# Rewriting the opening of a conditioned decoder trunk: half of the modulation in column groups on TensorE, splits off GpSimd, one queue of transfers, instructions in written order

## The chip, the cores and the metric

The kernel runs on one core of a Trainium2 chip. The time is device microseconds of one execution of the whole program. Five engines work side by side on their own queues: TensorE (PE; its weight loads are shown apart as PEld), VectorE (DVE), ScalarE (ACT), GpSimd (POOL) and SyncE (SP, which here only issues transfers).

## The reference

One layer with a sequence of 1024 and a width of 1024, all float32:

```
mod = silu(c) @ ada_w + ada_b            # (1, 3*1024): shift, scale, gate
h = rms_norm(x, norm_w) * (1 + scale) + shift
proj = h @ w_in                          # all inputs of both mixers
y_h = hgrn2_branch(...)                  # 8 heads, gated linear recurrence
y_g = gla_branch(...)                    # 4 heads, gated linear attention
merged = sigmoid(mg0) * (y_h @ w_branch0) + sigmoid(mg1) * (y_g @ w_branch1)
out = rms_norm(x + gate * (merged @ w_out), final_norm_w)
```

The change concerns only how the program begins: the shift and scale, `h`, and the first six column groups of `proj` (four of q, two of k of the linear attention).

## The kernel before

`h` is kept transposed: eight tiles, one for each group of 128 channels `d`, 1024 positions wide, worked on in two halves of 512 positions. Every product is split: a float32 operand is rounded to a high part (`hi`, a cast on ACT) and the rest (`lo`, a subtraction), and a matmul becomes three, hi·hi, lo·hi and hi·lo. One 128x128 by 128x512 matmul of these is called a product below.

The opening does this for the first half of the positions:

- `load_x` brings four tiles of x, `norm_x` squares them on ACT, takes the root, and scales them on DVE; `transpose_x(half, xs, d)` turns channel group d with four TensorE matmuls against `ident` into `pm`, and ACT copies the result into `hT`.
- `load_mod(d0, nd)` brings the columns of `ada_w` that make shift and scale of `nd` channel groups. There are five blocks, (0,1), (1,1), (2,2), (4,2), (6,2) as (first d, how many). `make_mod` multiplies each of the eight row groups k with the column `cs[:, k]` of silu(c) and adds them up on DVE into `acc` (which lies in the tile `scT`); matmuls with a column of ones then sum over the partitions, and DVE makes `modv` and `amul`. In block 0 the first four k are done by 128x1 matmuls on TensorE instead (`on_pe`).
- `make_h(half, d)` applies scale and shift on ACT in place, splits the result into `h_hi[d]` and `h_lo[d]`, and every second d stores a pair to DRAM from POOL's queue.
- `load_wg(k)` brings one row group of the six weight columns, 128x768, into one of three buffers in `xb`; `prep_wg` splits it into `wa_*` and `wb_*`, casts on ACT, subtractions on POOL.
- For each d, 18 products go into six PSUM banks `accs` (four in `pd`, two in `sc_ps`): 144 for the half. They are started once per bank at d = 0 and stopped at d = 7.

Then `make_ga(0)` makes a small projection with 16-column matmuls in four column groups, `qk_out` moves the six banks out on DVE, and `first_group` does the second half's 144 products, bank by bank, while the main stream of later projections begins. In `first_group`'s third step (`i == 2`) `make_ga(1)` runs and the side track `alpha_side` starts; the attention that needs its results starts when the fourth job's values are there.

Up to `norm_x(0)` the instructions of PE, ACT and DVE stand in the order in which the code is written (`manual_schedule`, left by `order.close()`). After it a scheduler places them on each engine. `S.get` and `S.free` hand out 46 slots of 4 KB a partition in turn, so a transfer can wait for the last reader of its slot.

Of the kernel before, what the change touches and what calls it, by code (L numbers as in the profile page):

```python
# [82 lines left out]
def hybrid_trunk_kernel(  # L83
# [37 lines left out]
    one_t = ones[:, 0:1]  # L121
    ones_r = cp.tile([P, P], F32R, name="ones_r")
# [40 lines left out]
    nc.vector.tensor_mul(cs, cs, vec[:, R_C:R_C + 8])  # L163

# [22 lines left out]
    def split(src, hi=None, lo=None, eng=None, pin=False):  # L187
# [4 lines left out]
        i = nc.scalar.copy(hi, src)  # L192
        if pin:
            tc.keep_in_program_order(i)
        (eng or nc.vector).tensor_sub(lo, src, hi.bitcast(F32))  # L195
        return hi, lo
# [23 lines left out]
    def make_h(half, d):  # L220
        b = hT[half, d // 2][:, d % 2, :]
        sl = slice(half * 512, half * 512 + 512)
        nc.scalar.activation(b, b, AF.Identity, bias=modv[:, 0, d:d + 1], scale=amul[:, d:d + 1])
        split(b, h_hi[d][:, sl], h_lo[d][:, sl])
        if d % 2:
            nc.gpsimd.dma_start(h_d[half][d // 2], hT[half, d // 2].rearrange("p a t -> p (a t)"))

    def load_mod(d0, nd):
        kq = 4 // nd
        parts = []  # L230
        for kk in range(KT // kq):
# [5 lines left out]
            parts.append(b)  # L237
        return parts

    def make_mod(d0, nd, parts, on_pe):  # L240
        kq = 4 // nd
        acc = scT_f[:, (d0 // 2 % 2) * 512:(d0 // 2 % 2) * 512 + 2 * nd * P].rearrange("p (a f) -> p a f", a=2)
        for k in range(on_pe, KT):
            src = parts[k // kq][:, k % kq]
            if k == on_pe:
                i = nc.vector.tensor_scalar_mul(acc, src, cs[:, k:k + 1])
                if on_pe:
                    tc.keep_in_program_order(i)
            else:
                nc.vector.scalar_tensor_tensor(acc, src, cs[:, k:k + 1], acc, ALU.mult, ALU.add)  # L250
        pm = mtile()
        for half in range(2):
            for i in range(nd):
                o = pm[:, half * nd + i:half * nd + i + 1]
                for k in range(on_pe):
                    nc.tensor.matmul(o, parts[k // kq][:, k % kq, half, i * P:(i + 1) * P], cs[:, k:k + 1],
                                     start=(k == 0), stop=False)
                nc.tensor.matmul(o, acc[:, half, i * P:(i + 1) * P], one_t, start=(on_pe == 0), stop=True)
        S.free(*parts)
# [17 lines left out]

    def load_wg(k):
        raw = xb_f[:, (k % 3) * 768:(k % 3) * 768 + 768]
        nc.sync.dma_start(raw, w_in[0, k * P:(k + 1) * P, C_GQ:C_GQ + NG * P])  # L280
        return raw

    def prep_wg(k, raw):
        split(raw[:, 0:512], wa_hi[k // 2][:, k % 2, :], wa_lo[k // 2][:, k % 2, :], nc.gpsimd, k < 2)
        split(raw[:, 512:768], wb_hi[k // 4][:, k % 4, :], wb_lo[k // 4][:, k % 4, :], nc.gpsimd, k < 2)
# [23 lines left out]
    blocks = [(0, 1), (1, 1), (2, 2), (4, 2), (6, 2)]  # L309
    mods, raws = {}, {}  # L310

    def load_mods(bi):
        mods[bi] = load_mod(*blocks[bi])

    def load_w(k):
        raws[k] = load_wg(k)

    for bi in range(3):
        load_mods(bi)
        load_w(bi)  # L320
    norm_x(0, x_t)
    vec_rows(rows_a, 24, R_SH)
    order.close()
    make_mod(0, 1, mods.pop(0), 4)
    transpose_x(0, x_t, 0)
    transpose_x(0, x_t, 1)
    acc0 = [dtile(), dtile()]
    accs = [acc0[f // 2][:, (f % 2) * 512:(f % 2) * 512 + 512] for f in range(4)]
    accs += [sc_ps[:, 0:512], sc_ps[:, 512:1024]]
    for bi, (d0, nd) in enumerate(blocks):  # L330
        if bi:
            make_mod(d0, nd, mods.pop(bi), 0)
        for d in range(d0, d0 + nd):
            make_h(0, d)
            prep_wg(d, raws.pop(d))
            if d + 3 < KT:
                load_w(d + 3)
            if d in (0, 2):
                load_mods(3 + d // 2)
            if d == 4:  # L340
                x_t2 = [load_x(t) for t in range(4, 8)]
            if d + 2 < KT:
                transpose_x(0, x_t, d + 2)
            if d == KT - 1:
                norm_x(1, x_t2)
            for f in range(NG):
                for n, (a, b) in enumerate(((0, h_hi), (1, h_hi), (0, h_lo))):
                    nc.tensor.matmul(accs[f], wg(a, d, f), b[d][:, 0:512],
                                     start=(d == 0 and n == 0), stop=(d == KT - 1 and n == 2))
# [9 lines left out]
    for d in range(KT):  # L359
        transpose_x(1, x_t2, d)  # L360
        make_h(1, d)

    def first_group():

        for f in range(NG):
            if f % 2 == 0:
                pd = dtile()
            ps = pd[:, (f % 2) * 512:(f % 2) * 512 + 512]
            for d in range(KT):
                for n, (a, b) in enumerate(((0, h_hi), (1, h_hi), (0, h_lo))):  # L370
# [1170 lines left out]
```

## Time and profile before

| What | Value |
|---|---|
| Times of three runs | 1249.24, 1251.12, 1251.75 us (median 1251.12) |
| Profiled execution | 1252.38 us, its span 1250.7 us |
| PE busy | 1205.7 us, 96% of the span |
| DVE, ACT, POOL busy | 61%, 42%, 11% |
| Transfers | 168.82 MB, mean 135 GB/s |
| Last product of the first half ends (L348) | 78.83 us |
| Last product of the second half starts (L371) | 127.9 us |

All times in a trace count from the start of the span. In a timeline row stand the start, the time taken, the engine, the line, the operation, out<-in by the program's names, how many instructions were merged, and in brackets the idle time before and what ended it. A busy PE is not PE at its peak: two matmuls in flight both count, so a row's time divided by its count is not the spacing, and the spacing is read from starts.

### The profile page before, as it was taken

What the parts mean: (1) busy time and instruction counts of PE and PEld (TensorE: products, weight loads), DVE (VectorE), ACT (ScalarE), POOL (GpSimd) and SP (SyncE); (2) the same over time, 40 slices, a digit from 0 to 9 for tenths busy, and PEclk for the clock granted to TensorE, in tenths of its full rate; (3) what the DMA queues carried; (4) which work ended last, traced back from release to release, by engine and by line L of the source; (5) the groups of instructions that cost most, each with busy time, mean ns of one, the idle gap of its engine ahead of it and who ended that gap; (6) DMA issues with size and microseconds to landing.
All of it is one profiled execution on the core that took longest, in us unless ns stands there. A gap on an engine that the chain in (4) does not pass through costs nothing.

```text
span 1250.7 us, 20782 instructions
## 1 busy us (share of the span) xinstructions
PE 1205.7 (96%) x8603; PEld 999.9 (80%) x8603; DVE 765.2 (61%) x1219; ACT 530.4 (42%) x784; POOL 132.4 (11%) x216
## 2 busy tenths in 40 slices
PE   4799999999999999999999999999999999998997
PEld 3676899989798888788887878877888888787786
DVE  5746425494857556777873365695422668979443
ACT  4467713343334344243332323456643644454222
POOL 5510000201211021021110101011110000000000
PEclk9899999999999999999999999999999999999999
DMA  8832100653644167255251212154546556235202
GB/s 269 278 115 86 52 18 18 217 188 102 203 143 144 63 208 254 92 179 174 96 177 45 60 41 68 38 183 169 173 163 225 179 171 201 83 100 170 118 34 101
DMA packets 126928, 168.82 MB, mean 135 GB/s; under 512 B 7019, under 2 KB 97185, under 8 KB 126834
## 3 DMA queue, kind: packets, MB, share of 16 engines
q1 hardware_dynamic: 115234, 129.53, 33.5%
q0 software_dynamic: 11552, 37.97, 7.8%
q8 instruction: 67, 1.10, 0.4%
q14 instruction: 27, 0.22, 0.1%
q10 hardware_dynamic: 48, 0.01, 0.0%
HBM read 125.53 MB, written 41.94 MB: 134 GB/s over the span
## 4 chain that ended last, share of the span: by engine, by line
PE 59%; issue 24%; DVE 8%; DMA 3%; POOL 2%; ACT 2%; SPq 1%; POOLq 0%; DVEq 0%; ACTq 0%
PE pd L454 13%; PE pd L1313 11%; PE sc_ps L1313 5%; PE pm L1313 5%; PE pd L556 2%; PE pd L557 2%; PE pd L558 2%; DVE scT L250 1%; PE pm L761 1%; PE pm L742 1%; PE pm L763 1%; PE pd L1083 1%; PE pd L1084 1%; PE pd L1085 1%; DVE b L195 1%
## 5 line engine op out<-in xcount | busy, mean ns | idle before, releaser
L454 PE MATMUL pd<-b,b 128*128 128x512 f32 x1632 | 386.3, 393 | 0.0
L454 PEld LDWEIGHTS pd<-b,b 128*128 128x128 f32 x1632 | 302.4, 188 | 64.0 <-issue 0.5
L1313 PE MATMUL pd<-b,b 128*128 128x512 f32 x720 | 175.7, 395 | 2.5 <-DVE b L866 1.5
L1313 PEld LDWEIGHTS pd<-b,b 128*128 128x128 f32 x720 | 134.7, 189 | 35.4 <-DVE b L866 1.9
L195 DVE TENSOR_TENSOR b<-b,b 128x1024 fp32r<-128x1024 f32 (+1 forms) x95 | 101.8, 1082 | 74.7 <-ACT b L192 34.8
L192 ACT CAST b<-b 128x1024 fp32r<-128x1024 f32 (+1 forms) x95 | 84.6, 904 | 104.0 <-DVE b L1169 14.7
L1256 DVE TENSOR_TENSOR b<-b,b 128x1024 fp32r<-128x1024 f32 x56 | 68.3, 1224 | 68.5 <-ACT b L1255 46.6
L1255 ACT CAST b<-b 128x1024 fp32r<-128x1024 f32 x56 | 58.5, 1051 | 62.8 <-PE pd L1313 17.2
L1313 PE MATMUL sc_ps<-b,b 128*128 128x512 f32 x324 | 79.0, 391 | 0.3 <-ACT scT L706 0.3
L1313 PE MATMUL pm<-b,b 128*128 128x512 f32 x300 | 72.5, 389 | 3.4 <-DVE b L1256 3.4
L513 PE MATMUL pd<-b,b 128*128 128x256 f32 x256 | 74.2, 290 | 0.0
L515 PE MATMUL pd<-b,b 128*128 128x256 f32 x256 | 72.5, 283 | 0.0
L514 PE MATMUL pd<-b,b 128*128 128x256 f32 x256 | 72.4, 283 | 0.0
L1313 PEld LDWEIGHTS sc_ps<-b,b 128*128 128x128 f32 x324 | 60.4, 188 | 13.6 <-ACT scT L706 0.8
L1313 PEld LDWEIGHTS pm<-b,b 128*128 128x128 f32 x300 | 56.3, 188 | 15.5 <-DVE b L1256 3.8
L1234 DVE TENSOR_TENSOR b<-b,b 128x1024 fp32r<-128x1024 f32 x36 | 45.1, 1263 | 18.1 <-ACT b L1233 10.3
L1171 POOL DMA_DIRECT2D ws<-b x64 | 34.6, 541 | 194.8 <-DVE b L1165 87.1
L556 PE MATMUL pd<-b,b 128*128 128x512 f32 x128 | 52.0, 406 | 0.0
L557 PE MATMUL pd<-b,b 128*128 128x512 f32 x128 | 50.4, 394 | 0.0
L558 PE MATMUL pd<-b,b 128*128 128x512 f32 x128 | 50.4, 394 | 0.0
L648 ACT COPY xb<-b 128x512 f32<-128x512 f32 x48 | 29.5, 620 | 49.3 <-PE sc_ps L628 26.3
L1233 ACT CAST b<-b 128x1024 fp32r<-128x1024 f32 x36 | 37.2, 1049 | 28.9 <-PE pd L1313 10.1
(268 smaller groups left out, 2041.9 us busy)
## 6 DMA issues: line engine op xcount, KB each, us to landing
b<-in_w_in_dram SPq DMA_DIRECT2D x66, 512.0 KB, 4.0
ws<-b POOLq DMA_DIRECT2D x64, 256.0 KB, 3.0
b<-ws SPq DMA_DIRECT2D x32, 512.0 KB, 4.2
b<-in_x_dram SPq DMA_DIRECT2D x16, 512.0 KB, 5.8
b<-in_ada_w_dram SPq DMA_DIRECT2D x32, 256.0 KB, 6.2
b<-in_w_branch_dram SPq DMA_DIRECT2D x16, 512.0 KB, 4.8
b<-h SPq DMA_DIRECT2D x14, 512.0 KB, 4.2
b<-in_w_in_dram SPq DMA_DIRECT2D x24, 256.0 KB, 3.5
```

The costliest lines, as they stand in the source:

```text
L192: i = nc.scalar.copy(hi, src)
L195: (eng or nc.vector).tensor_sub(lo, src, hi.bitcast(F32))
L454: nc.tensor.matmul(ps[0:w, th * 512:(th + 1) * 512], a[:, k, 0:w], b[:, th * 512:(th + 1) * 512], start=(k == 0 and n == 0), stop=(k == KT ...
L513: nc.tensor.matmul(o, lh, hi[:, k % 4, :], start=(k == 0), stop=False)
L514: nc.tensor.matmul(o, lh, lo[:, k % 4, :], start=False, stop=False)
L515: nc.tensor.matmul(o, ll, hi[:, k % 4, :], start=False, stop=(k == KT - 1))
L556: nc.tensor.matmul(o, lh, hi[:, k % 2, :], start=(k == 0), stop=False)
L557: nc.tensor.matmul(o, lh, lo[:, k % 2, :], start=False, stop=False)
L558: nc.tensor.matmul(o, ll, hi[:, k % 2, :], start=False, stop=(k == KT - 1))
L1255: nc.scalar.copy(hi, t)
L1256: nc.vector.tensor_sub(lo, t, hi.bitcast(F32))
L1313: nc.tensor.matmul(o, a[:, sl], c, start=(p in (1, 5) and kt == 0 and n == 0), stop=(kt == 3 and n == 2), skip_group_check=True)
```

## The change

1. `make_mod` is taken apart into `add_mod`, `mm_mod` and `end_mod`. DVE sums only k = 0 to 3. For k = 4 to 7, `mm_mod` runs four matmuls whose weights are 32 columns wide (`cs32`, silu(c) in column 0 and zeros elsewhere) and whose outputs stand in partitions 0, 32, 64 and 96 of one bank. `end_mod` adds that bank to `acc` on DVE; the matmul with ones sums over all partitions as before.
2. The blocks are (0,1), (1,2), (3,2), (5,2), (7,1).
3. The subtractions of `prep_wg` move from POOL to DVE.
4. Loads stand in one order: block 0, three raw weights, block 1, two raw weights in slots of their own, block 2, then further raw weights and blocks 3 and 4, then the second half of x.
5. The h stores of the first half all stand behind its products, those of the second inside `first_group`.
6. PE, ACT and DVE stay in written order through the whole first half: `mm_mod` and `end_mod` stand between groups of products of the block before, and `norm_x(1)` stands between block 4's `add_mod` and `mm_mod`. The first two channel groups of the second half are transposed and made before the last products of the first.
7. `first_group` goes through d outermost, with the transposes two d ahead, into the same banks `accs`; it has 24 steps as before, and `make_ga(1)` and `alpha_side` start at step 15.

```diff
+    cs32 = cp.tile([P, KT, 32], F32, name="cs32")
+    nc.gpsimd.memset(cs32, 0.0)
...
+    nc.vector.tensor_copy(cs32[:, :, 0], cs)
...
-        (eng or nc.vector).tensor_sub(lo, src, hi.bitcast(F32))
+        nc.scalar.copy(hi, src)
+        nc.vector.tensor_sub(lo, src, hi.bitcast(F32))
...
+    def store_h(half):
+        for i in range(4):
+            nc.gpsimd.dma_start(h_d[half][i], hT[half, i].rearrange("p a t -> p (a t)"))
...
+    blocks = [(0, 1), (1, 2), (3, 2), (5, 2), (7, 1)]
...
+    def add_mod(bi):
+        kq = 4 // blocks[bi][1]
+        acc = mod_acc(bi)
+        for k in range(4):
+            src = mods[bi][k // kq][:, k % kq]
+            if k == 0:
+                nc.vector.tensor_scalar_mul(acc, src, cs[:, k:k + 1])
             else:
                 nc.vector.scalar_tensor_tensor(acc, src, cs[:, k:k + 1], acc, ALU.mult, ALU.add)
...
+    def mm_mod(bi):
+        kq = 4 // blocks[bi][1]
+        w = 2 * blocks[bi][1] * P
+        mod_ps[bi] = mtile()
+        for j in range(4):
+            k = 4 + j
+            nc.tensor.matmul(mod_ps[bi][32 * j:32 * j + 32, 0:w], cs32[:, k, :],
+                             mods[bi][k // kq][:, k % kq].rearrange("p a f -> p (a f)"), start=True, stop=True)
+
+    def end_mod(bi):
+        d0, nd = blocks[bi]
+        acc = mod_acc(bi)
+        nc.vector.tensor_add(acc, acc, mod_ps.pop(bi)[:, 0:2 * nd * P].rearrange("p (a f) -> p a f", a=2))
...
-        split(raw[:, 0:512], wa_hi[k // 2][:, k % 2, :], wa_lo[k // 2][:, k % 2, :], nc.gpsimd, k < 2)
+        split(raw[:, 0:512], wa_hi[k // 2][:, k % 2, :], wa_lo[k // 2][:, k % 2, :])
...
-    order.close()
-    make_mod(0, 1, mods.pop(0), 4)
...
+    def product(half, d, f, n):
+        a, b = ((0, h_hi), (0, h_lo), (1, h_hi))[n]
+        nc.tensor.matmul(accs[f], wg(a, d, f), b[d][:, half * 512:half * 512 + 512],
+                         start=(d == 0 and n == 0), stop=(d == KT - 1 and n == 2))
...
     for bi, (d0, nd) in enumerate(blocks):
...
+        for d in ds:
             make_h(0, d)
+        if not more:
+            break
+        for d in nxt:
+            prep_wg(d)
+        add_mod(bi + 1)
+        if nd == 1:
+            for d in nxt:
+                transpose_x(0, x_t, d)
+            products(d0, (0, 1))
+            mm_mod(bi + 1)
+            products(d0, (2,))
+            end_mod(bi + 1)
+        else:
+            products(d0, (0, 1))
+            transpose_x(0, x_t, nxt[0])
+            if bi == 3:
                 norm_x(1, x_t2)
+            mm_mod(bi + 1)
+            products(d0, (2,))
+            for d in nxt[1:]:
+                transpose_x(0, x_t, d)
+            products(d0 + 1, (0,))
+            end_mod(bi + 1)
+            products(d0 + 1, (1, 2))
...
+    for d in range(2):
+        transpose_x(1, x_t2, d)
+    for d in range(2):
+        make_h(1, d)
+    products(KT - 1, (0,))
...
+    store_h(0)
     make_ga(0)
...
+        for d in range(KT):
+            if d + 2 < KT:
+                transpose_x(1, x_t2, d + 2)
+                make_h(1, d + 2)
...
+            for f in range(NG):
+                for n in range(3):
+                    product(1, d, f, n)
+                if d == KT - 1:
+                    qk_out(f, 1, accs[f])
+                if f % 2:
                     yield
...
-                if i == 2:
+                if i == 15:
                     make_ga(1)
                     start_side(alpha_side())
```

The order on DVE where block 0's modulation ends, before (`b_177` is block 0's second part, `b_181` block 1's first, `b_188` block 2's first; `pm_229` holds the sums over the partitions):

```order
L250 SCALAR_TENSOR_TENSOR scT<-b_177,cs,scT 128x256 x3
L246 TENSOR_SCALAR scT<-b_188,cs 128x512
L260 TENSOR_TENSOR modv<-pm_229,vec 128x2
L246 TENSOR_SCALAR scT<-b_181,cs 128x256
L262 SCALAR_TENSOR_TENSOR amul<-modv,vec 128x1
L250 SCALAR_TENSOR_TENSOR scT<-b_188,cs,scT 128x512
```

The same place now (`b_179` is block 0's first part, `pm_250` the bank of `mm_mod`, `b_188` block 1's first part, the others raw weights and h):

```order
L258 SCALAR_TENSOR_TENSOR scT<-b_179,cs,scT 128x256 x3
L274 TENSOR_TENSOR scT<-scT,pm_250 128x256
L281 TENSOR_TENSOR modv<-pm_256,vec 128x2
L283 SCALAR_TENSOR_TENSOR amul<-modv,vec 128x1
L196 TENSOR_TENSOR b_167<-xb,b_163 128x512
L196 TENSOR_TENSOR b_173<-xb,b_171 128x256
L196 TENSOR_TENSOR b_151<-b_239,b_143 128x512
```

A later block's sum no longer stands ahead of `modv` and `amul`; the subtractions of raw weights stand behind them instead.

The order on ACT at the end of the first half, before (`b_472` is hT of d = 6 and 7, `b_464` to `b_468` tiles of the second half of x):

```order
L223 ACTIVATE b_472<-b_472,modv,amul 128x512 x2
L192 CAST b_146<-b_472 128x512
L192 CAST b_147<-b_472 128x512
L192 CAST b_169<-xb 128x256
L203 ACTIVATE b_577,ssx<-b_464 128x1024
L203 ACTIVATE b_582,ssx<-b_466 128x1024
L205 ACTIVATE rsx<-ssx,eps_t 128x1 x2
```

Now (`pm_539` is the transposed d = 7, `b_480` its place in hT, `b_425` to `b_431` the second half of x, `b_150` is `h_hi[7]`):

```order
L217 COPY b_480<-pm_539 128x512
L204 ACTIVATE b_545,ssx<-b_425 128x1024
L206 ACTIVATE rsx<-ssx,eps_t 128x1
...
L204 ACTIVATE b_560,ssx<-b_431 128x1024
L206 ACTIVATE rsx<-ssx,eps_t 128x1
L224 ACTIVATE b_480<-b_480,modv,amul 128x512
L195 CAST b_150<-b_480 128x512
```

The four squares and roots of the second half of x moved from behind the last h of the first half to ahead of it.

More of the change, by code (lines that the diff above doesn't have):

```diff
@@ L185, in hybrid_trunk_kernel, with split @@
     amul = cp.tile([P, KT], F32, name="amul")
-    def split(src, hi=None, lo=None, eng=None, pin=False):
+    def split(src, hi=None, lo=None):
         if hi is None:
@@ L330, in hybrid_trunk_kernel @@
+    load_wg(3)
+    load_wg(4)
+    load_mod(2)
+    norm_x(0, x_t)
+    vec_rows(rows_a, 24, R_SH)
+    transpose_x(0, x_t, 0)
+    add_mod(0)
+    mm_mod(0)
+    end_mod(0)
+    prep_wg(0)
+    x_t2 = []
     for bi, (d0, nd) in enumerate(blocks):
-        if bi:
-            make_mod(d0, nd, mods.pop(bi), 0)
-        for d in range(d0, d0 + nd):
+        ds = range(d0, d0 + nd)
+        more = bi + 1 < len(blocks)
+        nxt = range(blocks[bi + 1][0], sum(blocks[bi + 1])) if more else ()
+        for d in ds:
```

115 lines of the change are left out of this document (46 added, 69 removed).

## The prediction

> **What bounds the kernel now.** I read the page first (span 1250.7), then busy time by stage (the windows), then the timeline of the opening, engine by engine.
>
> ```profile
> 24.80:31.70 6.90, 6.85 (x18) 4.84 (x18) 6.90 (x9) 2.08 (x5) 4.34 (x4) 1.00 0.56 153
> 31.70:38.20 6.50, 3.13 (x24) 2.61 (x24) 5.78 (x11) 3.50 (x8) 2.88 (x3) 0.89 0.95 325
> 38.20:43.50 5.30, 5.29 (x12) 3.79 (x13) 5.23 (x5) 4.02 (x8) 4.49 (x5) 0.50 0.42 111
> 43.50:53.40 9.90, 9.90 (x47) 8.18 (x45) 5.63 (x9) 0.93 (x2) 3.16 (x3) 1.00 1.06 350
> 53.40:60.60 7.20, 3.67 (x25) 3.19 (x24) 3.96 (x6) 4.61 (x9) 4.17 (x5) 0.76 0.78 307
> 60.60:64.00 3.40, 3.40 (x9) 2.72 (x10) 2.75 (x7) 3.27 (x7) 2.18 (x5) 0.50 0.52 181
> 64.00:78.80 14.80, 14.80 (x69) 11.94 (x72) 6.59 (x13) 4.95 (x13) 2.45 (x3) 1.00 0.11 40
> 78.80:128.10 49.30, 48.40 (x222) 33.17 (x222) 28.07 (x45) 36.79 (x49) 2.16 (x4) 1.00 0.39 119
> 128.10:1250.70 1122.60, 1102.16 (x8157) 922.68 (x8155) 690.89 (x1097) 458.92 (x667) 93.10 (x131) 0.99 0.40 129
> ```
>
> Columns: stretch and its length, busy PE, weight load, DVE, ACT, POOL, then granted clock, DMA share, GB/s. From 64.0 on PE is busy 98% or more, so what the opening gains moves the end by as much. The change rewrites the opening: the first half's 144 products (18 for each d) end at 78.83, though PE had two stretches with half its time idle (31.7 to 38.2 and 53.4 to 60.6), each followed by one at clock 0.50. The products' own rows show both speeds:
>
> ```profile
> 24.81 1.22 PE L348 MATMUL pd<-b,b 128*128 128x512 f32 x2 [1.62 <-ACT b L192]
> 26.26 4.25 PE L348 MATMUL pd<-b,b 128*128 128x512 f32 x10
> 30.34 1.32 PE L348 MATMUL sc_ps<-b,b 128*128 128x512 f32 x5
> 74.59 2.88 PE L348 MATMUL pd<-b,b 128*128 128x512 f32 x12
> 77.31 1.52 PE L348 MATMUL sc_ps<-b,b 128*128 128x512 f32 x6
> ```
>
> Twelve from 74.59 to 77.31: 0.227 us each, warm. Thirteen from 24.81, the first product, to 30.34 (one on `sc_ps` stands between the first two rows): 0.425, cold, though the clock column says 1.00 there. PE thus warms some 5.5 us after it starts, and each restart costs about 2.5 us. Why it waits:
>
> ```profile
> SPq L280 <- POOL b L195: 13.7, 2, 8.0
> 21.46 0.49 DVE L246 TENSOR_SCALAR scT<-b,cs 128x512 f32<-128x512 f32 x1 [5.21 <-DMA b<-in_ada_w_dram]
> 22.19 0.15 DVE L262 SCALAR_TENSOR_TENSOR amul<-modv,vec 128x1 f32<-128x1 f32 x1
> 24.98 9.85 DVE L250 SCALAR_TENSOR_TENSOR scT<-b,cs,scT 128x256 f32<-128x256 f32 x10
> 14.72 1.52 DVE L250 SCALAR_TENSOR_TENSOR scT<-b,cs,scT 128x256 f32<-128x256 f32 x3
> 55.44 1.59 ACT L192 CAST b<-xb 128x512 fp32r<-128x512 f32 x3 [9.37 <-DMA xb<-in_w_in_dram]
> ```
>
> SP's queue stood 13.7 us behind buffers that POOL still read. DVE took up block 2's sum, waited for its transfer until 21.46, and held block 0's short `amul` behind it. The modulation sums interleave while POOL subtracts: ten rows in 9.85 us (other shapes between) against 0.51 each with POOL idle. The last raw weights reached ACT at 55.44.
>
> **The change, part by part.** Prices from these rows:
>
> ```profile
> 0.00:24.80 24.80, 8.10 (x34) 6.76 (x34) 9.36 (x24) 11.37 (x22) 13.42 (x55) 1.00 0.99 302
> 26.76 0.93 ACT L192 CAST b<-xb 128x512 fp32r<-128x512 f32 x2 [1.21 <-DMA xb<-in_w_in_dram]
> 14.34 0.35 DVE L246 TENSOR_SCALAR scT<-b,cs 128x256 f32<-128x256 f32 x1 [1.83 <-DMA b<-in_ada_w_dram]
> 78.76 1.91 PE L304 MATMUL pm<-b,wga 128*16 128x512 f32 x16
> 16.30 0.59 PE L258 MATMUL pm<-ones,scT 128*128 128x1 f32 x2 [1.79 <-DVE scT L250]
> 33.84 0.58 PE L258 MATMUL pm<-ones,scT 128*128 128x1 f32 x4 [2.18 <-DVE scT L250]
> 85.43 0.44 PE pm L214 x4
> 36.90 1.54 DVE L250 SCALAR_TENSOR_TENSOR scT<-b,cs,scT 128x512 f32<-128x512 f32 x2
> 76.15 2.65 DVE L294 TENSOR_SCALAR b<-pd 128x512 f32<-128x512 f32 x4 [5.54 <-PE pd L348]
> 57.54 0.81 ACT L223 ACTIVATE b<-b,modv,amul 128x512 f32<-128x512 f32 x1 [0.51 <-DVE amul L262]
> 58.26 0.56 ACT L216 COPY b<-pm 128x512 f32<-128x512 f32 x1
> 58.73 0.62 ACT L192 CAST b<-b 128x512 fp32r<-128x512 f32 x1
> ```
>
> Transfers: 302 GB/s to 24.8 is 7.49 MB, which is the loads through the third raw weight; it is read at 26.76, 2.0 us later. With the queue full the rate is 0.35 MB/us (window 43.5 to 53.4). The new queue is the same bytes in another order: a load ending at B MB lands at 24.8 + (B - 7.49)/0.35 + 2.0. Block 1's modulation (6.42 MB) lands at 23.7, block 3's (12.19) at 40.2, the second half of x (15.73) at 50.3. The raw weights' buffers are given back by ACT and DVE near 22, before SP comes to refill them.
>
> The new `mm_mod`: four 512-wide float32 matmuls in column groups. The nearest row is `make_ga`, 16 passes (eight matmuls, 16 columns, four groups) in 1.91: one round 0.95 warm. In series it would be 3.4: four times two passes at 0.427, since eight take that. I take the row, it has the same groups; half for 256 wide, double when cold. The Trainium skill, TensorEngine Tiling (Key Properties), states that changing the tiling mode drains the engine; no figure is given, so the price of a switch comes in a rival below.
>
> Block 0: its second part lands at 14.3. Then `mm_mod` cold 0.95, the sum's add 0.4 (half of 2.65/4 for 512 wide from PSUM), the two ones-matmuls 0.59, `modv` and `amul` 0.4 with their gaps, make_h's activation and cast 1.6 with gaps, and 0.6 of handovers: first product at 18.9 instead of 24.81.
>
> Block 1: 12 cold products to 24.0, `mm_mod` (its data came at 23.7) warm 0.95, six warm products 1.4, ones-matmuls 0.58: 27.0. DVE, which first splits three raw weights, adds four rows of at most 0.77 by 24.9, in time. `modv`, `amul`, activation, cast: 2.1 of bare PE wait. h of d=1 is there at 29.1.
>
> From 29.1 PE is fed. A block of two d costs PE 36 products 8.2, two transposes 0.9, `mm_mod` 0.95, ones 0.6: 10.6. Against it DVE has ten 512-wide rows' worth (two splits of h, two raw weights of one and a half each, four of the sum, one add), at most 7.7 at 0.77; ACT two copies, two activations, two casts and two raw weights, 5.9; the transfers 2.88 MB, 8.2. So PE hides all three, POOL's former subtractions on DVE among them; were DVE's cover of 2.9 gone, each further us would cost one.
>
> The new wait is near the end: `norm_x(1)` now stands ahead of block 4's modulation on ACT and on DVE, and block 4's ones-matmul stands in PE's queue ahead of 30 products.
>
> ```profile
> 8.59 1.06 ACT L203 ACTIVATE b<-b 128x1024 f32<-128x1024 f32 x1 [0.91 <-DMA b<-in_x_dram]
> 11.14 0.29 ACT L205 ACTIVATE rsx<-ssx,eps_t 128x1 f32<-128x1 f32 x1
> 11.66 0.75 DVE L207 TENSOR_SCALAR b<-b,rsx 128x1024 f32<-128x1024 f32 x1
> ```
>
> PE transposes d=7 after 84 products, five transposes, two `mm_mod` and two ones: 29.1 + 24.3 = 53.4. ACT copies it by 54.0; four squares with their roots, two of which took 8.59 to 11.43, take 5.7: 59.7; DVE scales by 60.7 and adds by 61.1. PE has had its last free work at 56.6: 4.6 us idle. Ones to 61.8, then 12 products. Cold they take 5.1, warm 2.7. After the idle stretches of before the gate shut 5.1 us (0.89 over 31.7 to 38.2 is 1.4 us at half) and 3.7 us (0.76 over 53.4 to 60.6) after dense work ended; 4.6 lies between, and both old ones ended cold. I take cold: 66.9, two transposes 0.9, 18 products 4.1, end of the last 0.2: the first half ends at **72.1** against 78.83, **6.7** earlier. The Trainium skill, TensorE: Matmul & The Clock Gate (Part 1), gives a free-running window of about 3.4 us, so 4.6 us of idle may or may not hold a whole one; a shut gate is then not certain, which the range allows for.
>
> The second half:
>
> ```profile
> 83.77 1.66 PE L371 MATMUL pd<-b,b 128*128 128x512 f32 x6
> 147.46 1.06 ACT L857 ACTIVATE b<-b 128x1024 f32<-128x1024 f32 x1
> 180.23 1.31 PE L596 MATMUL sc_ps<-xb,b 128*32 128x80 f32 x64
> 226.77 8.14 SPq L1133 DMA_DIRECT2D b<-h  x5
> ```
>
> Before, its first product came 4.94 us after 78.83, of which 1.91 `make_ga` and 1.3 three transposes: 1.7 wait. Now two transposes are already done (**0.9**), and the wait is 0.8, for DVE to split two h tiles and clear `make_ga`'s bank (ACT's 4.1 us of copies and casts after the transposes, then two splits and a memset): **0.9** less. The rest of the half is the same work, PE at 98%. The alpha side starts 13 steps later, at 1.4 to 2 us a step some 18 to 26 us; its last step was at 147.46, the first scores at 180.23, so 33 us cover it. The h stores on POOL, all after the first half now, are first read at 226.77. The added memset on POOL, the copy of `cs` on DVE (both under 0.3 beside transfers) cost nothing.
>
> Sum: 6.7 + 0.9 + 0.9 = **8.5**. The profiled execution took 1252.38 (span 1250.7), 1.3 above the median 1251.12; on the median, 1251.12 - 8.5 = **1242.6**.
>
> **Rivals.**
> 1. The clock stays open over the 4.6 us: 2.4 more, **1240.2**. For it: 4.6 is less than the 5.1 of one old gap. Against it: the other shut after 3.7. Chance 0.17.
> 2. Less gain: PE waits at one or two more written places, each with a cold restart of 2.5, the first candidate the 2.1 us at 27.0. One gives **1245.1**, two 1247.6, three with short stalls 1250. For it: a fixed order can't fill a gap with what is ready. Against it: 2.2 us idle at 31.66 left the rows at 33.84 at warm price. Chance 0.13.
> 3. Slower: the column groups run in series and PE drains at each switch. In series 2.5 more for each of blocks 0 to 3 (block 4's lies in the idle stretch): 9.9. A drain is bounded by the gap in the weight loads between groups,
>
> ```profile
> 79.20 0.12 PEld L304 LDWEIGHTS pm<-b,wga 128*16 128x16 f32 x4 [0.31 <-issue]
> ```
>
> 0.31, twice a block: 2.5. Together 12.4: **1255.0**. It decides once the groups cost 8.5 more than reckoned. Against it: the 1.91 row, which has four groups at once and starts right at the end of a full-width product. This is the way in which the Trainium skill's drain would speak against the change; the trace shows no such gap there. Chance 0.05.
> 4. It doesn't do what it says: SP still stops for some 13.7 us on a buffer. Block 3 lands at 54 instead of 40.2, PE needs it at 43.0: 11 late, **1253.7**. Against it: the buffers are free some 10 us early. Chance 0.05.
>
> **How the numbers follow.** My forecast 1242.6 has 0.60. The range goes from rival 1 without the 0.8 wait, 1239.4, to rival 2 with three restarts, 1250: it leaves out 3 and 4 and a tenth for what I have not seen. Faster by over 0.2% (below 1248.6; 0.2% is about what a measurement here can tell): 0.60 + 0.17 + half of rival 2, 0.83. Within 0.2%: the rest of rival 2 0.06 and 0.01 of the others, 0.07. Slower: 3 and 4, 0.10.
>
> **What would show it.** Right: first product near 19; PE dense from 29 to 56; an idle gap before block 4's ones-matmul, which waits for DVE behind `norm_x(1)`, then clock 0.50; last product of the first half near 72; the first product of the second some 3 us later; `mm_mod` groups of 0.95. Wrong: `mm_mod` groups of 3 us, SP waiting for DVE or PE for many us, or a second half longer than 49.3.

## Result and the profile after

The changed kernel takes 1243.49 us (median of six runs, 1241.94 to 1243.85) against 1250.82: a ratio of 0.995, interval 0.9936 to 0.9963. The profiled execution took 1243.66 (span 1242.0). On a second chip, beside the kernel before, it came to 0.9968 (0.9954 to 0.9981; 1245.12 against 1249.53). So the gain is 4 to 7 us where 8.5 was forecast; the time lies in the range given. Runs of one kernel spread by up to 8.8 us, those of the kernel before mostly with the clock that they were granted (correlation -0.70 to -0.78 on three chips), so kernels are compared below by their ratio to the kernel before on the same chip.

Busy time by stage of the changed kernel (columns as in the prediction):

```profile
18.00:24.00 6.00, 5.97 (x20) 3.82 (x20) 5.22 (x9) 2.59 (x6) 0.00 (x0) 1.00 1.08 365
24.00:28.40 4.40, 2.46 (x18) 2.09 (x14) 1.01 (x3) 1.41 (x3) 0.34 (x1) 1.00 1.10 348
28.40:59.20 30.80, 30.73 (x156) 23.37 (x156) 18.80 (x36) 16.50 (x32) 3.87 (x8) 0.94 0.82 282
59.20:64.40 5.20, 1.16 (x7) 0.88 (x5) 3.08 (x7) 2.83 (x7) 0.35 (x1) 0.90 0.22 61
64.40:69.70 5.30, 5.30 (x14) 4.03 (x15) 1.01 (x3) 1.43 (x2) 1.50 (x2) 0.50 0.25 102
69.70:75.10 5.40, 5.40 (x29) 4.59 (x28) 1.38 (x2) 3.75 (x6) 0.54 (x1) 0.95 0.00 0
75.10:123.00 47.90, 45.11 (x216) 32.50 (x214) 22.29 (x39) 29.66 (x38) 1.59 (x3) 1.00 0.35 110
```

PE is dense from 28.4 to 59.2, idle for most of 59.2 to 64.4, cold to 69.7, and is through with the first half at 75.1, against 78.83 before. PE's timeline, the rows that answer to the steps of the prediction:

```profile
18.03 2.08 PE L343 MATMUL pd<-b,b 128*128 128x512 f32 x4 [0.20 <-ACT b L195]
...
22.45 0.63 PE L343 MATMUL sc_ps<-b,b 128*128 128x512 f32 x2
23.01 1.07 PE L268 MATMUL pm<-b,cs 128*32 128x512 f32 x8
24.01 1.21 PE L343 MATMUL pd<-b,b 128*128 128x512 f32 x4
...
28.47 1.43 PE L343 MATMUL pd<-b,b 128*128 128x512 f32 x4 [2.01 <-ACT b L195]
29.70 1.05 PE L343 MATMUL sc_ps<-b,b 128*128 128x512 f32 x2
...
63.55 0.98 PE L278 MATMUL pm<-ones,scT 128*128 128x1 f32 x4 [4.04 <-DVE scT L274]
64.40 2.05 PE L343 MATMUL pd<-b,b 128*128 128x512 f32 x4
...
77.59 2.58 PE L343 MATMUL pd<-b,b 128*128 128x512 f32 x10
...
118.78 0.96 PE L343 MATMUL pd<-b,b 128*128 128x512 f32 x3 [2.59 <-DVE b L322]
```

The column groups run side by side: `mm_mod` takes 1.07 and starts as the two products from 22.45 end. At 28.47 PE waited 2.0 for d=1's cast, and the products behind are cold from the fourth on (1.05 for two, against 0.62 warm). The 4.04 ahead of 63.55 is the gap behind `norm_x(1)`; DVE's rows show it directly, the last scaling of x and then at once the add that PE waits for:

```profile
62.32 0.75 DVE L208 TENSOR_SCALAR b<-b,rsx 128x1024 f32<-128x1024 f32 x1
62.99 0.41 DVE L274 TENSOR_TENSOR scT<-scT,pm 128x256 f32<-128x256 f32 x1
...
117.43 0.69 DVE L908 TENSOR_SCALAR b<-b 128x1024 f32<-128x1024 f32 x1 [2.29 <-ACT b L906]
118.04 0.68 DVE L322 TENSOR_SCALAR b<-pd 128x512 f32<-128x512 f32 x1
```

The last two rows are a wait that the prediction did not have. In the second half's last d, DVE stands at the first operation of alpha's second head (L908) until ACT delivers, the eviction of f=0 queues behind it, and PE's three products of f=1, in the same two-bank tile, wait 2.59.

The second profile of the same program puts the stages at the same places (second half's first product at 78.04 instead of 77.59), but the clock elsewhere:

```profile
29.17 2.07 PE L343 MATMUL pd<-b,b 128*128 128x512 f32 x4 [2.01 <-ACT b L195]
...
65.52 0.58 PE L278 MATMUL pm<-ones,scT 128*128 128x1 f32 x4 [4.04 <-DVE scT L274]
65.96 1.96 PE L343 MATMUL pd<-b,b 128*128 128x512 f32 x4
...
68.57 1.51 PE L343 MATMUL pd<-b,b 128*128 128x512 f32 x4
69.92 0.62 PE L343 MATMUL sc_ps<-b,b 128*128 128x512 f32 x2
```

Here d=1's products are cold from the first, and those at 65.96 are warm after some 3 us, where the first profile's stayed cold for the whole 5.3.

### The profile page after: what moved, and what is told of

The parts are those of the page before. It is cut to its first block, busy times and chain, and to the rows that moved or that the text cites. A ratio compares the mean times of both kernels' runs of the same rounds, so it can differ in the third digit from the quotient of the medians.

```text
span 1242.0 us, 20840 instructions
## 1 busy us (share of the span) xinstructions
PE 1202.8 (97%) x8627; PEld 996.6 (80%) x8627; DVE 759.9 (61%) x1225; ACT 535.3 (43%) x786; POOL 115.7 (9%) x201
## 4 chain that ended last, share of the span: by engine, by line
PE 59%; issue 23%; DVE 8%; DMA 4%; ACT 3%; POOL 2%; SPq 0%; POOLq 0%; DVEq 0%; ACTq 0%
PE pd L518 14%; PE pd L1377 9%; PE sc_ps L1377 5%; PE pm L1377 4%; PE pd L343 3%; PE pd L620 2%; PE pd L621 2%; PE pd L622 2%; PE sc_ps L343 1%; DVE b L196 1%; PE pm L825 1%; PE pd L1147 1%; PE pd L1148 1%; PE pd L1149 1%; DMA b<-yh 1%
## 5 line engine op out<-in xcount | busy, mean ns | idle before, releaser
L518 PEld LDWEIGHTS pd<-b,b 128*128 128x128 f32 x1632 | 302.4, 188 | 64.3 <-issue 0.7
L1377 PEld LDWEIGHTS pd<-b,b 128*128 128x128 f32 x720 | 134.4, 189 | 35.7 <-DVE b L930 1.9
L196 DVE TENSOR_TENSOR b<-b,b 128x1024 fp32r<-128x1024 f32 (+2 forms) x99 | 102.5, 1045 | 92.0 <-ACT b L195 75.3
L195 ACT CAST b<-b 128x1024 fp32r<-128x1024 f32 (+2 forms) x99 | 86.7, 888 | 109.1 <-PE pd L518 16.9
L1319 ACT CAST b<-b 128x1024 fp32r<-128x1024 f32 x56 | 58.4, 1050 | 65.3 <-PE pd L1377 19.1
L1377 PEld LDWEIGHTS pm<-b,b 128*128 128x128 f32 x300 | 56.6, 189 | 15.6 <-DVE b L1320 3.7
L343 PE MATMUL pd<-b,b 128*128 128x512 f32 x192 | 56.6, 431 | 4.8 <-DVE b L322 2.6
L1298 DVE TENSOR_TENSOR b<-b,b 128x1024 fp32r<-128x1024 f32 x36 | 45.1, 1262 | 18.1 <-ACT b L1297 10.3
L343 PEld LDWEIGHTS pd<-b,b 128*128 128x128 f32 x192 | 37.3, 203 | 17.2 <-issue 3.4
```

The lines of the kernel that those rows point to most:

```text
L196: nc.vector.tensor_sub(lo, src, hi.bitcast(F32))
L343: nc.tensor.matmul(accs[f], wg(a, d, f), b[d][:, half * 512:half * 512 + 512], start=(d == 0 and n == 0), stop=(d == KT - 1 and n == 2))
L518: nc.tensor.matmul(ps[0:w, th * 512:(th + 1) * 512], a[:, k, 0:w], b[:, th * 512:(th + 1) * 512], start=(k == 0 and n == 0), stop=(k == KT ...
L1319: nc.scalar.copy(hi, t)
L1377: nc.tensor.matmul(o, a[:, sl], c, start=(p in (1, 5) and kt == 0 and n == 0), stop=(kt == 3 and n == 2), skip_group_check=True)
```

## The experiments

All edits are to the changed kernel unless said otherwise. The last column is the start of the first half's last product in the profile (78.44 in the kernel before). The intervals reach 1.5 to 2.8 us to each side; where two edited runs lie closer than that, the rows carry the argument and not the times.

| Run | Ratio to before, 95% | us | First half's last product |
|---|---|---|---|
| changed (again) | 0.995 (0.9968) | 1243.49 (1245.12) | 74.72 (75.15) |
| e1 norm later | 0.9918, 0.9896 to 0.994 | 1240.15 | 67.47 |
| e9 spare products | 0.9934, 0.9914 to 0.9954 | 1241.08 | 69.89 |
| e2 evictions after | 0.9955, 0.994 to 0.997 | 1244.01 | 75.84 |
| e8 old second half | 0.9995, 0.9981 to 1.001 | 1249.30 | 73.71 |
| e11 old opening, new second half | 1.0009, 0.9997 to 1.0021 | 1250.42 | 81.10 |
| e12 three edits | 1.0036, 1.0022 to 1.005 | 1253.63 | 66.93 |
| e13 norm later, spare | 0.9908, 0.9887 to 0.9929 | 1238.98 | 67.47 |
| e4 groups in series | 1.0034, 1.0021 to 1.0048 | 1253.66 | 83.25 |
| e5 modulation on DVE | 1.0008, 0.9995 to 1.0021 | 1251.22 | 77.33 |
| e6 splits on POOL | 0.9973, 0.996 to 0.9986 | 1246.73 | 76.39 |
| e7 scheduler | 0.994, 0.9922 to 0.9957 | 1242.47 | 71.13 |

**The control** (the changed kernel again).

> The changed kernel itself, unaltered, beside the three that follow: the first experiments ran on a chip on which the kernel before took 1248.94 instead of 1250.82, so small differences need a control of their own. Expected: a ratio to the kernel before of 0.995. From the first profiles of five kernels that share this opening, the 12 products of d=1 behind the 2.0 us idle stretch were cold three times and warm once, and the clock opened 1.8 to 4.4 us after the first product: if that depends on a phase that differs from run to run and not on the program, this profile differs from the earlier one of the same program by up to 1.7 us at one of these places. If the program fixes it, the clock changes at the same products as before (open at the 11th product, shut at d=1's fourth, open 5.5 us later).

The clock's changes moved between two profiles of one program, as shown above: when it changes is the run's, not the program's.

**The gap before block 4: the wait and the clock.** First the wait is taken away:

```diff
-            if bi == 3:
-                norm_x(1, x_t2)
             mm_mod(bi + 1)
...
             products(d0 + 1, (1, 2))
+            if bi == 3:
+                norm_x(1, x_t2)
```

> The normalisation of the second half of x stands behind the 12 last products of d=6, and no longer ahead of block 4's modulation. Theory (DVE's queue behind norm_x(1) made the gap at 59.2 to 63.6, and the gap made the cold products after it): DVE adds mm_mod's bank at about 57.4, the ones-matmul of block 4 follows the products without a stop at 59.2, the clock stays 1.00, and only about 1.0 us is waited for the activation of d=7, which still stands behind the four squares on ACT (to 62.1). First half's last product near 68.5 instead of 75.1; make_ga then waits about 1.2 for DVE, so 5.5 of the 6.5 reach the end: 1238.0 (changed kernel: 1243.5). Rival A (only the queue counts, the clock does not open: PE is cold for another reason): the products stay at 0.42, the half ends near 71, 1240. Rival B (what the opening gains is lost again in the attention): 1243.5.

PE's timeline:

```profile
28.98 1.21 PE L343 MATMUL pd<-b,b 128*128 128x512 f32 x4 [2.01 <-ACT b L195]
...
58.30 0.50 PE L278 MATMUL pm<-ones,scT 128*128 128x1 f32 x4
58.67 1.17 PE L343 MATMUL pd<-b,b 128*128 128x512 f32 x4
...
63.00 0.76 PE L215 MATMUL pm<-ident,b 128*128 128x128 f32 x5 [0.53 <-DVE b L208]
```

The ones-matmul follows at 58.30 without a stop, the products stay warm, two waits for DVE's scaling of 0.8 together are left, and the half ends 7.2 to 7.7 earlier than in the two profiles of the changed kernel. In this run d=1's products were warm after the same 2.01 us of idle, which is 1.6 to 2.4 of that. By the ratios the edit is worth 4.0 (against 0.995) to 6.2 (against 0.9968), and the profile's span, 1234.2 against 1242.0 and 1243.0, loses nothing of the gain later: the theory. The time, 1240.15, is the one that rival A named, but that rival has the products cold at 0.42, and the rows show them warm.

Then the wait is kept and only filled:

```diff
             products(d0, (2,))
             end_mod(bi + 1)
+            spare(6)
...
             products(d0 + 1, (0,))
+            if bi == 3:
+                spare(14)
             end_mod(bi + 1)
```

> Nothing is moved; PE gets work without use in the two stretches in which it waits: 6 products into a PSUM bank that nobody reads behind block 1's ones-matmul (2.0 us idle before d=1), and 14 ahead of block 4's ones-matmul (4.0 us idle). Theory (the cold clock after a pause costs 1.7 us at d=1 and 2.6 us at 64.4, apart from the pause itself): both times the 12 products that follow take 2.7 us instead of 4.45 and 5.3, the pauses' ends stay where they were (the second 1.7 earlier, since all before it is), and the first half ends near 70.8 instead of 75.1: 1239.2 for 4.3 less. Rival A (the products are slow there for another reason, as reading operands just written): they stay slow, 1243.5 or 0 to 1 more. Rival B (the clock opens only after some 5 us of dense work, which 1.4 us of spare products in the first pause don't give): the first stretch stays cold, the second opens partly, 1241 to 1242.5.

```profile
26.20 1.64 PE L369 MATMUL pm<-b,b 128*128 128x512 f32 x6
28.35 1.20 PE L343 MATMUL pd<-b,b 128*128 128x512 f32 x4 [0.51 <-ACT b L195]
...
57.61 3.33 PE L369 MATMUL pm<-b,b 128*128 128x512 f32 x14
61.82 0.58 PE L278 MATMUL pm<-ones,scT 128*128 128x1 f32 x4 [0.87 <-DVE scT L274]
62.26 1.17 PE L343 MATMUL pd<-b,b 128*128 128x512 f32 x4
```

Both groups behind are warm (1.17 to 1.20 for four), the waits end as before, and the half is 4.8 to 5.3 earlier, 2.0 to 4.2 by the ratios. So useless work in a wait buys what the shut clock cost. Behind the 4.04 pause this stands against five profiles that were cold there (both of the changed kernel, e2, e6, e8); behind the 2.0 pause it shows less, since e1 was warm there without it. Rivals A and B are out.

**The wait on f=0's eviction.**

```diff
-                if d == KT - 1:
-                    qk_out(f, 1, accs[f])
                 if f % 2:
                     yield
+        for f in range(NG):
+            qk_out(f, 1, accs[f])
```

> The second half's results are taken out of PSUM (qk_out) only behind its last products in program order; in the changed kernel the three products of f=1 for d=7 stood on PE behind DVE's eviction of f=0 and waited 2.6 us at 116.2. Theory (that wait is on the path): no product of the second half waits for DVE, the half's products end near 117.5, the next block's first product waits under 1 us for the two evictions of its PSUM tile, and 2.0 to 2.6 reach the end: 1241.2. Rival A (the attention's own waits on DVE take it back): 1243.5. Rival B (the eviction of f=0 and f=1 is only later, and the next block waits as long for its tile): 1243.5, with a wait of over 2 us on that block's first product.

```profile
122.06 10.31 PE L518 MATMUL pd<-b,b 128*128 128x512 f32 x37 [2.29 <-DVE b L322]
```

Rival B: no product of the half waits, but the next block's first waits 2.29 for its tile, because DVE still stands at L908 first. The ratio is unchanged. The order on DVE is the cause, not the order on PE: in e12 below, which moves the evictions as here but starts alpha seven steps later, the next block's first product (109.16) waits for nothing.

**Groups side by side or in series** (they add up in one group of columns; `acc` gets only its first 32 partitions from the bank, the sum is the same).

```diff
-            nc.tensor.matmul(mod_ps[bi][32 * j:32 * j + 32, 0:w], cs32[:, k, :],
+            nc.tensor.matmul(mod_ps[bi][0:32, 0:w], cs32[:, k, :],
```

> The four modulation matmuls of a block go to the same 32 columns and add up there, one after another, instead of into four column groups. Theory (groups run side by side: eight passes of 512 in 1.07 us): in series the eight take about 3.4, so 2.4 more for each of blocks 1 to 3 and 1.2 to 2.4 for block 0, block 4's 1.2 shifts the normalisation behind it too: 9 to 11 more at the end of the first half, which the later stages don't give back, 1253 or ratio 1.003. Rival (they run in series already, or the pass is not what costs): rows of 1.07 as now, ratio 0.995. Drains at a switch of the column groups, if they cost anything, go with the groups: the products behind would start up to 0.3 earlier.

```profile
25.45 3.62 PE L268 MATMUL pm<-b,cs 128*32 128x512 f32 x8
29.00 1.20 PE L344 MATMUL pd<-b,b 128*128 128x512 f32 x4
```

3.62 instead of 1.07. The product behind starts 0.07 before the row's end in both kernels, so no price of the change between groups shows. The half ends 8.1 later than in the control, where 9 to 11 were expected; the ratio is 0.0066 higher, 8.3 us.

**All the modulation on DVE.**

```diff
-        for k in range(4):
+        for k in range(KT):
...
-        for j in range(4):
+        for j in range(0):
...
-        nc.vector.tensor_add(acc, acc, mod_ps.pop(bi)[:, 0:2 * nd * P].rearrange("p (a f) -> p a f", a=2))
```

> All eight rows of the modulation are summed on DVE again, no matmuls in column groups; the written order and the transfers stay as changed. Theory (TensorE's half takes PE 1.07 a block and spares DVE four rows of 0.51 to 0.78 less the add of 0.69): block 0's first product 0.6 to 1.0 later, block 1's h 1.3 later (3.1 of rows behind the last transfer instead of 1.07 and 0.69), then DVE has about 10 us of work a block against 9.5 for PE, so PE waits 0 to 2 more by block 3; PE saves 1.07 in blocks 2 and 3. Together 1 to 3 longer than the changed kernel, ratio 0.997 to 0.999. Rival A (DVE becomes the bound with rows of 0.78): 5 to 8 longer, 1.000 or more. Rival B (the half on TensorE is worth nothing, the order and the transfers do it all): 0.995 or less.

PE's waits between 18 and 82 (in total, times, longest):

```profile
PE pm L276 <- DVE scT L258: 6.1, 3, 2.7
PE pd L341 <- ACT b L195: 3.2, 3, 2.0
```

Against the control 5.0 us longer by the ratio (5 to 7 with both results of the changed kernel), rival A's figure: the ones-matmuls wait 6.1 for DVE's sums in three places, and behind the two long waits (2.6 and 2.7) the products are cold. Without TensorE's half nothing of the change's gain is left; the same holds of e8 below, so such prices can't be added up.

**The splits on POOL again.**

```diff
-        nc.vector.tensor_sub(lo, src, hi.bitcast(F32))
+        (eng or nc.vector).tensor_sub(lo, src, hi.bitcast(F32))
```

> The low parts of the raw weights are subtracted on POOL again (1.15 us each instead of 0.5 to 0.7 on DVE). Theory (DVE has slack from 29 on, but its rows beside POOL's run at the price of before, 0.985 instead of 0.51 to 0.78): DVE's sums stretch by 0.2 to 0.4 a row, block 1's h comes 0.5 to 1.5 later, and the blocks of two d stay hidden: 0 to 2 longer than the changed kernel, ratio 0.996 to 0.998. Rival A (POOL's subtractions and the stretched rows make DVE late for each block's ones-matmul, with a cold restart each): 4 or more longer, 1.000. Rival B (taking POOL out of the opening brought nothing): the same time, DVE's rows as long as now.

Block 1's three rows on DVE, here and in the changed kernel:

```profile
22.22 3.93 DVE L258 SCALAR_TENSOR_TENSOR scT<-b,cs,scT 128x512 f32<-128x512 f32 x3
```

```profile
21.01 2.33 DVE L258 SCALAR_TENSOR_TENSOR scT<-b,cs,scT 128x512 f32<-128x512 f32 x3
```

1.31 against 0.78 each beside POOL. Still the half ends only 1.2 later than in the control, and the ratio gives 0.6 to 2.9 us: the slack on DVE took it, as the theory had it.

**The order left to the scheduler** (`order.close()` moved ahead of the first half's transposes).

> The same operations and transfers, but the scheduler orders them from the first transposes on, as it did before; its PE order takes the ones-matmuls of blocks 2 and 3 some products later and lets only 12 products stand between the squares of x's second half and block 4's ones-matmul. Theory (the written order was needed since the scheduler's order holds block 0's sum behind the raw weights' subtractions on DVE): first product 1 to 3 later, the other stretches about as written, the gap ahead of block 4 about as long (4): 1 to 3 longer, ratio 0.997 to 0.999. Rival A (the order does not matter once the transfers don't stop): the same as the changed kernel, 0.996. Rival B (the scheduler fills the gap before block 4, which the written order can't): 2 to 4 shorter, 0.993.

```profile
30.16 1.17 PE L343 MATMUL pd<-b,b 128*128 128x512 f32 x4
...
63.18 0.50 PE L278 MATMUL pm<-ones,scT 128*128 128x1 f32 x4
63.55 1.17 PE L343 MATMUL pd<-b,b 128*128 128x512 f32 x4
```

and on DVE:

```profile
60.46 0.42 DVE L274 TENSOR_TENSOR scT<-scT,pm 128x256 f32<-128x256 f32 x1 [0.18 <-PE pm L268]
60.80 0.75 DVE L208 TENSOR_SCALAR b<-b,rsx 128x1024 f32<-128x1024 f32 x1
```

Theory and rival A are both wrong: the first product comes at 30.16, 10.7 later than in the control, and yet the half ends 4.0 earlier, since PE never stops after that and stays warm. That is rival B, 1.2 to 3.5 us by the ratios: the scheduler put the add that PE waits for (L274) ahead of the last two scalings of x, and twelve products cover it. The written order was not what made the change faster; it carried the gap.

**The second half.** Old, bank by bank, behind the new opening:

```diff
+    for d in range(2, KT):
+        transpose_x(1, x_t2, d)
+        make_h(1, d)
...
-                if i == 15:
+                if i == 2:
```

> The opening stays as changed; the second half goes back to bank by bank (six transposes and their h ahead of all products, new PSUM tiles, alpha and make_ga(1) from the first steps on). Theory of the prediction (the second half is the same work, the new one starts with 0.9 less wait): 1243.5 + 0.9 minus the 2.6 us wait on f=1, which has no counterpart there, minus nothing later: 1241.8. Rival (the later 3.8 us that the changed kernel gained over the one before, of which about 2.2 lie in the first two heads' attention, come from where alpha's work and the h stores now stand): these waits come back, 1.4 + 1.4 instead of 0.6 before the scores, and it is 1244 to 1246. A second half that costs several us more than the new one (PE below 95% busy in it) would say that the change's gain sits there: above 1247.

New, behind the old opening (an edit to the kernel before):

```diff
-    for d in range(KT):
+    for d in range(2):
         transpose_x(1, x_t2, d)
         make_h(1, d)
...
-                if i == 2:
+                if i == 15:
```

> The complement of the run with the second half bank by bank: the opening of the kernel before (scheduler's order, all modulation on DVE, POOL's subtractions), with the new second half (d outermost in the six banks of the first half, h made two d ahead, alpha and make_ga(1) from the 16th step). Theory (what the changed kernel gains up to the end of the first half is 3.7, at the start of the second half 2.5 more, and the rest comes from where alpha and the evictions now stand): the second half's first product comes 3.2 after the last of the first instead of 5.3, and the end is 2 to 4 earlier than before, ratio 0.997. Rival A (the second half is worth nothing by itself): 1.000. Rival B, by the medians of the run with the old second half, which left nothing of the gain (0.9995): all of it is the second half's, 0.995.

Neither alone is faster than before. e8 is 3.4 longer than the control by the ratio (5.6 against the first 0.995): more than the prediction's 0.9 and than the rival's 0.5 to 2.5; and e11 is its rival A. But the rival's reason does not hold. PE's largest waits in the attention (123 or 128 to 680), in the kernel before, then with the old second half (e8), then with the new one behind the old opening (e11):

```profile
PE sc_ps L628 <- DVE tot L631: 1.4, 1, 1.4
PE sc_ps L683 <- DVE blk L672: 1.4, 1, 1.4
```

```profile
PE sc_ps L662 <- DVE xb L658: 0.9, 1, 0.9
```

```profile
PE sc_ps L684 <- DVE blk L673: 1.2, 1, 1.2
```

All that are listed there make 4.3 before, 1.9 and 2.6 in the changed kernel's two profiles, 1.8 in e8 and 3.2 in e11; the other profiles with the new opening and an unmoved alpha lie between 1.5 (e6) and 3.0 (e13). If they go with anything, it is the new opening, and then by 0.2 to 2.8 us.

Part of e8's loss is in its own second half. Its expectation gave the changed kernel's wait for an eviction no counterpart there, but PE waits for one (77 to 124):

```profile
PE pd L437 <- DVE b L322: 2.3, 2, 2.1
```

From its first product to the next stage's this half takes 46.8 (77.03 to 123.87), where the one before, without such a wait, took 44.3; so of a lead of 6.7 over the kernel before 4.2 are left. In e11's profile the opening, unaltered, ended 2.7 later than in the profile before (81.10 against 78.44), with a granted clock of 0.82 instead of 0.88 from 24 on: there the clock hides what the edit does.

One thing is plain: the second half's first product, 5.3 behind the last one of the first before, is 5.35 behind it in e11 and 3.3 in e8 (rows' starts), so that gain needs the transposes which only the new opening makes early. The rest is not settled: the two ratios make 1.0004 together, the changed kernel has 0.995 to 0.9968. In its profile e8's next stage is only 0.7 behind the changed kernel's, though its clock opened sooner; its other runs were up to 6 us longer than the profiled one, and of those there is no trace.

**Towards a faster version.** Three edits:

```diff
-            products(d0, (2,))
-            end_mod(bi + 1)
+            for f in range(NG):
+                if f == 3:
+                    end_mod(bi + 1)
+                product(0, d0, f, 2)
+            spare(3)
...
+                if i == 22:
                     start_side(alpha_side())
```

with `norm_x(1)` moved as in e1 and the evictions as in e2.

> The changed kernel with three edits: the normalisation of x's second half behind the products of d=6; block 1's ones-matmul three products earlier, with three spare products of no use behind the other three; alpha's chain on DVE and ACT from the 23rd step of the second half instead of the 16th, with the evictions behind the last products. Theory: 1240.15 of the first edit alone (0.9918 of the kernel before), less 0.7 for the shorter wait before d=1 and up to 1.7 for its clock, less 2.2 for the wait on f=0's eviction, which alpha's two operations held up on DVE: 4 less, ratio 0.989. Rival (alpha, now some 12 us later, is late for the first head's scores): the wait comes back there and it is at 0.992 or above.

The first half ended 8 earlier, and the run was one of the two slowest. PE's waits from 123 to 680, and two windows:

```profile
PE sc_ps L700 <- DVE tot L703: 12.3, 3, 5.9
```

```profile
250.00:260.00 10.00, 6.25 (x82) 4.78 (x81) 9.86 (x27) 3.44 (x6) 0.00 (x0) 0.83 0.16 54
560.00:570.00 10.00, 4.10 (x77) 3.24 (x76) 5.48 (x16) 0.40 (x1) 0.54 (x1) 0.84 0.75 267
```

That is the rival's loss and more, but not in its place: the first head's scores wait for nothing, and PE waits 12.3 for DVE's products of decays at three later heads (near 250, 465 and 565), with the clock shut around the stops. Without the moved alpha and evictions:

> The run with three edits without the third: the normalisation behind the products of d=6, block 1's ones-matmul three products earlier and three spare products behind the other three; alpha's chain and the evictions stand as in the changed kernel. Theory (the later alpha was what cost: it put DVE's products of decays late, PE waited 12.3 us on them in three stops and was cold after each): those waits are gone, the second half keeps the 2.2 us wait on f=0's eviction, and the ratio to the kernel before is 0.991, 0.9918 of the first edit alone less up to 0.7 us before d=1 and up to 1.7 us where d=1's products would have been cold. Rival (the opening's gain itself, over 10 us, is what the attention can't take, since DVE is as late as before): waits in the attention as with three edits, ratio above 1.000.

0.9908, 1238.98 us: the lowest of all, faster than both kernels, though its interval overlaps those of e1 and e9. Its stops at that line are down from 12.3 to 1.5. If the moved evictions cost nothing, as in e2, alpha's start seven steps later cost 16 us by the ratios (14.7 by the medians). The heads' scores do start some 5 us later in e12 (the first at 174.2 against 169.3, the second at 242.9 against 237.9); why DVE is late at just those three heads stays open.

## Why the prediction was right, and where it was not

- **First product 18.9.** It came at 18.03, in the other runs with the same start at 18.1 to 19.5 (20.1 with the splits on POOL, e6). Right.
- **Column groups.** Side by side at 1.07, as `make_ga`'s row had said (0.95); e4 shows the price in series, 8.1 at the half's end where rival 3 had 9.9. The Trainium skill, TensorEngine Tiling (Key Properties), has a change of tiling mode drain the engine; `mm_mod` starts at 23.01 as the product before it ends, and the four products behind it take 1.21, about 0.1 over the usual, as behind transposes and ones-matmuls; a larger drain does not show in the rows.
- **PE hides DVE from 29.1.** PE was dense, but this stretch took 31.0 us (28.47 to 59.5, which is 63.55 less the gap) where I had 27.5 (29.1 to 56.6). This is the mis-sized term: the first half ended at 75.1, not 72.1, so it gave 3.7, not 6.7. Of the 3.5 too little, 1.7 are d=1's cold products after 2.0 idle, the place that rival 2 named for its one restart. The rest is mostly small change that the price of 0.227 a product left out, as these rows of the dense stretch show:

```profile
49.00 0.95 PE L278 MATMUL pm<-ones,scT 128*128 128x1 f32 x8
49.81 1.19 PE L343 MATMUL pd<-b,b 128*128 128x512 f32 x4
...
51.30 1.09 PE L343 MATMUL pd<-b,b 128*128 128x512 f32 x4
```

  Four products behind another kind of matmul take 1.17 to 1.20, otherwise 1.09 or less, at seven places of this stretch; and a block of two d has eight ones-matmuls, 0.81 from start to start, where I took the four of 0.58.
- **The gap.** Right in cause (DVE behind `norm_x(1)`, shown by e1), in length (4.04 against 4.6) and in the shut clock (5.3 for 12 products against 5.1; e9). The size is the run's: in the control's profile they take 4.4.
- **Start of the second half.** 1.8 was forecast; 77.59 against 83.77 makes 6.2 with the first half's 3.7, so 2.5. Right in kind.
- **The second half is the same work.** Nearly: 2.6 of new wait at 118.78, and the lead at the next stage is 5.0 of the 8.5.
- **The end.** The profiled lead is 8.7 all the same: 2.4 of waits in the attention are gone, and the profile of before holds one stretch more of shut clock near 660, worth about 1.7 (0.83 over 10 us). So the two profiles agree with 8.5 by terms that made up for each other, which I had not foreseen; that is luck, and the repeated runs say 4 to 7. Nor was what the opening gained carried along unchanged: the lead was 6.2 at the second half's start, 5.0 a stage later and 8.7 at the end.
- **Alpha covered by 33 us.** Wrong as an argument: the last alpha and the first scores are not the only link. In e12 the first scores wait for nothing, and still seven further steps cost some 15 us (e12 against e13) at later heads. In the program the side track is a queue, so every head behind alpha moves too; that this is the whole chain is argued and not shown. That the start which the change chose was safe was luck.

The Trainium skill, TensorE: Matmul & The Clock Gate (Part 1), has a window of about 3.4 us that runs on its own. The runs agree that the moment depends on the run and not on the program: the same 2.01 us pause left d=1 warm in e1 and cold in the control. The size fits as well: from 59 to 76 the granted clock is 0.80 in the first profile and 0.90 in the control, which is 6.8 and 3.4 us at half, about two such windows and one. What does not fit is the length of the pause: 2.01 us, shorter than a window, was enough in most runs.

## What to carry to other kernels

A producer of the next stage's input shouldn't stand ahead of the current stage's last link in a queue: moving `norm_x(1)` by twelve products was worth about as much as the whole rewrite (4.0 to 6.2 us against 4 to 7). PE gains less from starting early than from not stopping: e7 began 10.7 us later and ended the half 4 us sooner. A chain off the path can have a start from which later work on its engines is late, so move it in small steps and read the waits of the later stages.

## What the hardware showed that was not expected

- A 512-wide row of DVE's sums takes 0.78 with POOL idle, as forecast (0.77), and 1.31 beside POOL's subtractions (e6), 1.7 times as long. The Trainium skill, SBUF — State Buffer (SBUF: two separate sides), describes a port pair that the two engines lock in turn; the rows agree that POOL slows DVE; the size is theirs and not the page's.
- A pause of 2.0 us after 0.95 of sparse ones-matmuls can shut the clock: it did in the changed kernel's two profiles and in e2, e4, e6 and e8, in e1 it did not. The wait of 2.2 to 2.6 on f=0's eviction did so too in e2, e9 and e13 (granted clock 0.83 from 110 to 120 in e9), but not in the changed kernel, the control and e1.
- With six spare products in that pause, or three and an earlier ones-matmul (e12, e13), it stayed open, at no cost that shows. Since e1 was open without them, the 14 in the 4.04 us pause are the better evidence.
